# Two head groups of values behind one stationary operand, in a two-layer encoder trunk

## The chip, the cores and the metric

The kernel runs on one core of one Trainium2 chip. The metric is the time of one execution in microseconds (us): the median of several runs, and the lower the better. A profile of one execution stands beside it. Busy times, waits and the granted clock of TensorE come from that profile.

## What is computed

The reference is a bidirectional encoder of two layers with D_MODEL = 1024. It is run on two request groups that share all weights: 512 sample tokens and 256 prompt tokens, 768 columns together. Each layer projects the normalised input with one wide matrix and runs three token mixers on the result.

```python
z = h @ w_in
cq, ckv, kr, gate_a, qkv_b, gate_b, qkv_c, gate_c, merge = jnp.split(z, cuts, axis=-1)
o_a = mla_attention(cq, ckv, kr, g_q, w_uq, g_kv, w_ukv)
o_b = dilated_attention(rope(q_b, pos), rope(k_b, pos), v_b)   # three head groups, dilation 1, 4, 16
o_c = neighbourhood_attention(q_c, k_c, v_c, rpb)              # 8 heads on a grid 64 wide
mixed = mg[0] * (o_a * silu(gate_a)) @ w_pa + mg[1] * ... + mg[2] * ...
x = x + gate * rmsnorm(mixed @ w_out, g_post)
```

The change concerns the values of branch B (three head groups of four heads, so three times 256 columns of `w_in`) and of branch C (eight heads, taken as two groups of four, so twice 256 columns).

## The kernel before, in words

All matrix products are made in three passes of split operands: hi times hi, hi times lo, lo times hi. Activations `h` lie in SBUF as [feature, token], in eight tiles of 128 features (k = 0 to 7), each in a hi and a lo part. `feat_mm` (line 180) projects with the weights as stationary operand, and so yields features by tokens. One such projection is 8 x 3 x 2 = 48 matmuls, 24 with 512 columns (sample) and 24 with 256 (prompt).

Values are needed as tokens by features, so `value_group` (line 709) turns the roles round: 128 tokens are the stationary operand, and a group's 256 weight columns stream past. A group is 8 k x 6 token tiles x 3 passes = 144 matmuls (line 722). Six token tiles share three accumulators of 512 columns, two to one. `tok` picks the 128 tokens of a tile. For branch B with dilation 1 they are neighbours (`tok_b`, line 736). With dilation 4 and with dilation 16 they are every fourth token of the sample, or every second one of the prompt. These two picks are the same, since `strided` takes its step from the request group and not from the dilation. For branch C `tok_c` (line 886) has ScalarE write column-major copies `hc` of each k's hi and lo (line 893), 32 copies for one group, and the tiles are slices of these.

`load_split` (line 160) fetches 1024 weight columns and splits them: a ScalarE cast gives hi (line 175), a subtraction on VectorE or GpSimd gives lo (line 158). `store_v` (line 690) empties an accumulator into slots of tag `cv`: for each piece a ScalarE cast to hi (line 696), then a VectorE subtraction to lo (line 697). A group fills four slots, and there are 14 (`BUFS`, line 77). `vslice` (line 699) reads them in the products of probabilities and values (o_ps, lines 671, 859 and 872).

The projection accumulators come from pool `ps_mm`: three tiles of tag g0 and three of tag g1 may be in use at a time (`PS`, line 46). `feat_mm` takes one of each, `value_group` two g0 and one g1.

In a layer, `branch_a`, `branch_b`, `branch_c`, `merge` and `project` are traced in this order. `branch_b` makes its three value groups first (line 761). `branch_c` makes its first one before head pair 0 and the second before head pair 2 (line 924). The framework's planner then fixes the order of each engine's instructions by a simulation of its own, taking whatever is ready. So the tail of one branch runs mixed with the start of the next, and projections fill the time in which a softmax waits. `early` (line 990) adds merge gates as more such filling, by a table written by hand (`FILL`).

Of the kernel before, what the change touches and what calls it, by code (L numbers as in the profile page):

```python
# [11 lines left out]
F32 = mybir.dt.float32  # L12
F32R = mybir.dt.float32r
# [7 lines left out]
P = 128  # L21
D = 1024
KT = 8
NS, NP_ = 512, 256
# [36 lines left out]


@with_exitstack
def trunk_kernel(ctx, tc, x_t, c_row, c_col, w_ada0, w_ada, cols, w_a, w_feat, w_val, w_uqk, w_qr, w_uv, w_pj, w_o,
                 bias_s, bias_p, rope_t, rope_k, mask_b, mask_c, y_t):
    nc = tc.nc
    depth = w_feat.shape[0]
# [638 lines left out]
            s, c = b + 1, 256 + hd * 128  # L706
        return slots[s][:, c:c + 128]

    def value_group(l, idx, tok):

        slots = [U("cv", F32R, name="vb") for _ in range(4)]
        acc = [ps_mm.tile([P, NS], F32, tag=tag, name="vp") for tag in ("g0", "g0", "g1")]
        parts = []
        for k in range(KT):
            if k % 4 == 0:
                parts = load_split(w_val[l, idx, k // 4], 1024)[1]
            wh, wl = parts[(k % 4) // 2]
            ws = slice((k % 2) * 256, (k % 2) * 256 + 256)
            tk = tok(k)
            for t in range(6):  # L720
                for i, (a, w) in enumerate(((0, wh), (0, wl), (1, wh))):
                    nc.tensor.matmul(acc[t // 2][:, (t % 2) * 256:(t % 2) * 256 + 256], tk(t, a), w[:, ws],  # L722
                                     start=(k == 0 and i == 0 and t % 2 == 0),
                                     stop=(k == KT - 1 and i == 2 and t % 2 == 1))
        for t in range(6):
            store_v(slots, t, acc[t // 2][:, (t % 2) * 256:(t % 2) * 256 + 256])
        return slots


# [28 lines left out]
    def branch_b(l, h, hl):  # L758
        state["phase"] = "b"
        cos_b, sin_b = rope_tables(1)  # L760
        vb = [value_group(l, i, tok_b(h, d)) for i, d in enumerate((1, 4, 16))]
        o_t = None
        for hd in range(4):
            e = hd % 2
# [152 lines left out]

    def branch_c(l, h, hl):
        state["phase"] = "c"
        vc = None  # L920
        for pr in range(4):
            early(l, hl, FILL[l][13 + 2 * pr])
            if pr % 2 == 0:
                vc = value_group(l, 3 + pr // 2, tok_c(h))
            qo = feat_mm(w_feat[l, F_C + pr * 2], KT, hl, name="qc")
            qs2 = [q_stack(lambda g: qo[g], e, perm_cq, 0.125) for e in range(2)]
            ko = feat_mm(w_feat[l, F_C + pr * 2 + 1], KT, hl, name="kc")
# [319 lines left out]


def _value_tiles(w_in):
    starts = [1184 + 1536 + 256 * g for g in range(3)] + [3744 + 1024 + 256 * g for g in range(2)]  # L1250
    L = w_in.shape[0]
    out = [w_in[:, :, s:s + 256].reshape(L, 2, 4, P, 256).transpose(0, 1, 3, 2, 4).reshape(L, 2, P, 1024)
           for s in starts]
    return np.stack(out, 1)


def _chunk(w, cols):
# [62 lines left out]
def _layout(i):  # L1320
# [11 lines left out]
    uqn, uqr = uq[..., :64].reshape(L, 384, 512), uq[..., 64:].reshape(L, 384, 256)  # L1332
    uk, uv = ukv[..., :64].reshape(L, 256, 512), ukv[..., 64:].reshape(L, 256, 512)
    r = np.arange
    wuqk = np.stack([np.concatenate([_chunk(uqn, r(128) + 128 * j), _chunk(uk, r(128) + 128 * j)], 2)
                     for j in range(4)], 1)
    wqr = np.stack([_chunk(uqr, r(128) + 128 * j) for j in range(2)], 1)
# [7 lines left out]
    def spread(t):  # L1345
# [7 lines left out]
    mb, mc = _masks()  # L1353
    rope = _rope_tables()
    return dict(x_t=xt, c_row=crow, c_col=ccol, w_ada0=wada0, w_ada=wada, cols=colv.transpose(2, 0, 1), w_a=a["w_in"][:, :, :NA].reshape(L, KT, P, NA), w_feat=_feature_tiles(a["w_in"]),
                w_val=_value_tiles(a["w_in"]), w_uqk=wuqk, w_qr=wqr, w_uv=wuv, w_pj=wpj, w_o=wo,
                bias_s=bs, bias_p=bp, rope_t=rope, rope_k=_rope_rows(rope), mask_b=mb, mask_c=mc)


_NAMES = ["x_t", "c_row", "c_col", "w_ada0", "w_ada", "cols", "w_a", "w_feat", "w_val", "w_uqk", "w_qr", "w_uv", "w_pj", "w_o",  # L1360
          "bias_s", "bias_p", "rope_t", "rope_k", "mask_b", "mask_c"]


# [18 lines left out]
```

## Time and profile before

| | before |
|---|---|
| median of 3 runs | 2030.2 us (2030.12 to 2031.44) |
| the profiled execution | 2033.65 us |
| its span, first to last instruction | 2031.9 us |
| TensorE matmul busy | 1899.3 us, 93% |
| VectorE busy | 1548.6 us, 76% |
| ScalarE busy | 1066.2 us, 52% |
| mean granted TensorE clock | 0.977 |

A matmul's end is modelled in these profiles and the busy time of neighbours overlaps, so the pace of a run of matmuls is read from the starts: the time from the first start to the start of what follows, divided by their number. PE is the matmul, PEld the load of the stationary operand, DVE VectorE, ACT ScalarE, POOL GpSimd. In a window's row the granted clock of 1.00 is full speed and 0.50 the lower level.

### The profile page before, as it was taken

The numbers are of one execution on the slowest core, as the hardware profiler recorded it, in microseconds if no ns is written. First come the engines' busy times: TensorE is split into PE (matmuls) and PEld (weight loads), VectorE is DVE, ScalarE is ACT, GpSimd is POOL, SyncE is SP. The second block draws the span as 40 slices with busy tenths as digits, with TensorE's granted clock in tenths as the row PEclk, the third lists the DMA queues.
The fourth block names the chain that finished last, engine by engine and source line by source line (L and its number), as shares of the span: only waits on it lengthen the run. The fifth ranks groups of instructions, "written<-read, shape, count | busy, mean of one in ns | idle before, by whom it ended". The sixth has DMA issues, their size and how long they took to land.

```text
span 2031.9 us, 31377 instructions
## 1 busy us (share of the span) xinstructions
PE 1899.3 (93%) x11250; PEld 1706.7 (84%) x11250; DVE 1548.6 (76%) x3016; ACT 1066.2 (52%) x2185; POOL 641.3 (32%) x428
## 2 busy tenths in 40 slices
PE   7999899999989888999699999999999989898998
PEld 6987789988778777887699888889987878887898
DVE  8557787389978889799986258787489968888763
ACT  5456474256695855222264356574365586855241
POOL 6304334012113334125722014352012212434570
PEclk9999999999999998999899999999999999899999
DMA  8232231232312233557432242421232322233652
GB/s 286 72 115 67 92 110 57 71 93 76 96 43 71 89 123 104 176 168 263 154 117 72 88 129 85 134 77 59 73 91 73 99 66 86 82 112 107 207 176 76
DMA packets 94541, 220.28 MB, mean 108 GB/s; under 512 B 17984, under 2 KB 32392, under 8 KB 94384
## 3 DMA queue, kind: packets, MB, share of 16 engines
q1 hardware_dynamic: 89776, 211.97, 32.0%
q10 hardware_dynamic: 4608, 6.29, 1.1%
q8 instruction: 89, 1.46, 0.3%
q14 instruction: 68, 0.56, 0.1%
HBM read 172.73 MB, written 28.18 MB: 99 GB/s over the span
## 4 chain that ended last, share of the span: by engine, by line
PE 57%; DVE 25%; ACT 7%; issue 6%; DMA 3%; POOL 2%; SPq 0%; ACTq 0%; DVEq 0%; POOLq 0%
PE mg L199 14%; PE vp L722 8%; PE op L1133 6%; PE qkb L199 5%; PE pp L1032 5%; PE gate L199 4%; DVE fixed L158 3%; DVE fixed L309 3%; ACT hc L893 3%; PE cq L547 2%; DVE fixed L668 2%; PE sp L632 2%; PE ck L547 2%; PE o_ps L671 2%; DVE tq L658 1%
## 5 line engine op out<-in xcount | busy, mean ns | idle before, releaser
L653 POOL PARTITION_ALL_REDUCE fixed<-fixed x128 | 305.2, 2416 | 545.4 <-DVE fixed L650 325.7
L199 PE MATMUL mg<-fixed 128*128 128x512 f32 (+1 forms) x2304 | 433.2, 339 | 0.4 <-DVE kb L418 0.4
L199 PEld LDWEIGHTS mg<-fixed 128*128 128x128 f32 x2304 | 357.4, 189 | 49.8 <-PE sp L953 0.6
L175 ACT CAST fixed<-fixed 128x512 fp32r<-128x512 f32 (+1 forms) x332 | 199.6, 607 | 346.5 <-PE mg L199 106.6
L158 DVE TENSOR_TENSOR fixed<-fixed,fixed 128x512 fp32r<-128x512 f32 (+3 forms) x309 | 230.0, 747 | 147.2 <-ACT fixed L175 142.0
L199 PE MATMUL qkb<-fixed 128*128 128x512 f32 (+1 forms) x1152 | 211.3, 338 | 0.0
L199 PEld LDWEIGHTS qkb<-fixed 128*128 128x128 f32 x1152 | 176.4, 188 | 23.9
L199 PE MATMUL gate<-fixed 128*128 128x512 f32 (+1 forms) x960 | 185.1, 343 | 6.7 <-DVE fixed L158 4.0
L1032 PE MATMUL pp<-hi,fixed 128*128 128x512 f32 (+1 forms) x640 | 165.2, 346 | 20.3 <-DVE fixed L158 7.3
L199 PEld LDWEIGHTS gate<-fixed 128*128 128x128 f32 x960 | 150.7, 192 | 28.4 <-DVE fixed L158 4.5
L722 PE MATMUL vp<-fixed 128*128 128x256 f32 x864 | 154.6, 333 | 0.0
L722 PEld LDWEIGHTS vp<-fixed 128*128 128x128 f32 x864 | 153.1, 255 | 1.7
L1032 PEld LDWEIGHTS pp<-hi,fixed 128*128 128x128 f32 x640 | 113.8, 194 | 38.3 <-DVE fixed L158 9.4
L668 DVE TENSOR_TENSOR fixed<-tq,fixed 128x512 fp32r<-128x512 f32 (+1 forms) x160 | 130.6, 840 | 2.7 <-ACT fixed L667 2.4
L309 DVE SCALAR_TENSOR_TENSOR fixed<-tm,fixed 128x768 f32<-128x768 f32 (+1 forms) x128 | 109.1, 852 | 2.5 <-DMA tm<-in_w_ada_dram 0.4
L1032 PE MATMUL pp<-lo,fixed 128*128 128x512 f32 (+1 forms) x320 | 110.2, 345 | 0.0
L1133 PE MATMUL op<-wo,fixed 128*128 128x384 f32 (+1 forms) x648 | 107.9, 320 | 1.0 <-DVE fixed L1106 1.0
L659 ACT ACTIVATE tq<-tq 128x512 f32<-128x512 f32 (+1 forms) x160 | 82.6, 545 | 49.2 <-DVE tq L658 48.5
L893 ACT CAST hc<-fixed 128x512 fp32r<-128x512 f32 (+1 forms) x128 | 104.6, 894 | 0.2
L1133 PEld LDWEIGHTS op<-wo,fixed 128*128 128x128 f32 x648 | 102.1, 189 | 1.3 <-DVE fixed L1106 1.3
L658 DVE TENSOR_TENSOR tq<-tq,fixed 128x512 f32<-128x512 f32 (+1 forms) x160 | 98.1, 661 | 4.9 <-POOL fixed L653 4.5
L424 POOL MEMSET kb<- 64x768 f32 x56 | 41.1, 736 | 191.1 <-PE sp L790 58.2
(242 smaller groups left out, 3872.2 us busy)
## 6 DMA issues: line engine op xcount, KB each, us to landing
fixed<-in_w_feat_dram SPq DMA_DIRECT2D x108, 512.0 KB
tm<-in_w_ada_dram SPq DMA_DIRECT2D x42, 384.0 KB
th_scr<-the SPq DMA_DIRECT2D x35, 384.0 KB
th<-th_scr SPq DMA_DIRECT2D x35, 384.0 KB
fixed<-in_w_val_dram SPq DMA_DIRECT2D x20, 512.0 KB
xs<-xb SPq DMA_DIRECT2D x96, 96.0 KB
fixed<-in_w_pj_dram SPq DMA_DIRECT2D x32, 256.0 KB
fixed<-in_w_o_dram SPq DMA_DIRECT2D x16, 512.0 KB
```

What stands on the lines that cost most here:

```text
L158: eng.tensor_sub(out, a, b)
L175: nc.scalar.copy(hi[:, :m], raw[:, o:o + m])
L199: state["mm"] = nc.tensor.matmul(outs[g], w[:, wsl], a[g], start=(i == 0 and wi == 0), stop=(i == nk - 1 and wi == 2))
L309: nc.vector.scalar_tensor_tensor(junk, x, 1.0, c, ALU.mult, ALU.mult, accum_out=ada2[:, l, i, g, j:j + 1])
L653: nc.gpsimd.partition_all_reduce(red, out, P, RED.max if op == ALU.max else RED.add)
L658: nc.vector.tensor_sub(x, x, m)
L659: nc.scalar.activation(x, x, AF.Exp)
L668: nc.vector.tensor_sub(lo, x, f(hi))
L722: nc.tensor.matmul(acc[t // 2][:, (t % 2) * 256:(t % 2) * 256 + 256], tk(t, a), w[:, ws], start=(k == 0 and i == 0 and t % 2 == 0), stop=( ...
L893: nc.scalar.copy(x[:, o:o + n].rearrange("p (c r) -> p c r", r=rows), colmajor(f(h[i][g][:, k]), rows))
L1032: nc.tensor.matmul(pp, w[:, ws], o[k][a][:, o_:o_ + n], start=(i == 0), stop=(i == 3 * nk - 1))
L1133: mm = nc.tensor.matmul(op[cc], m[a][g][:, k, c0:c0 + P], parts[k][cc][b], start=(k == 0 and i == 0), stop=(k == KT - 1 and i == 2))
```

## The change

The values of the dilation-4 and dilation-16 groups of branch B are projected together, and so are the two groups of branch C. A new function, `value_pair`, streams 512 weight columns past each stationary operand and takes all six tiles of `ps_mm`, one for each token tile. Its weights come as a new array, in four loads of 1024 columns (two k of 512) where two groups had two loads each (four k of 256). The dilation-1 group keeps `value_group`. In branch C both groups are made before head pair 0, from one set of `hc` copies, and eight `cv` slots are filled then.

```diff
+    def value_pair(l, which, tok):
+
+        slots = [[U("cv", F32R, name="vb") for _ in range(4)] for _ in range(2)]
+        acc = [ps_mm.tile([P, NS], F32, tag=tag, name="vp") for tag in ("g0", "g0", "g0", "g1", "g1", "g1")]
+        parts = []
+        for k in range(KT):
+            if k % 2 == 0:
+                parts = load_split(w_val2[l, which, k // 2], 1024)[1]
+            wh, wl = parts[k % 2]
+            tk = tok(k)
+            for t in range(6):
+                for i, (a, w) in enumerate(((0, wh), (0, wl), (1, wh))):
+                    nc.tensor.matmul(acc[t], tk(t, a), w, start=(k == 0 and i == 0), stop=(k == KT - 1 and i == 2))
+        for t in range(6):
+            for j in range(2):
+                store_v(slots[j], t, acc[t][:, j * 256:j * 256 + 256])
+        return slots
...
-        vb = [value_group(l, i, tok_b(h, d)) for i, d in enumerate((1, 4, 16))]
+        vb = [value_group(l, tok_b(h, 1))] + value_pair(l, 0, tok_b(h, 4))
...
-        vc = None
+        vcs = None
         for pr in range(4):
             early(l, hl, FILL[l][13 + 2 * pr])
-            if pr % 2 == 0:
-                vc = value_group(l, 3 + pr // 2, tok_c(h))
+            if pr == 0:
+                vcs = value_pair(l, 1, tok_c(h))
+            vc = vcs[pr // 2]
```

The host lays the same weight columns out in the two arrays `w_val` and `w_val2`. The numbers computed are the same.

## Rows read from the trace of the kernel before

**Rows 1.** The page: TensorE's share, then busy tenths and granted clock in 40 slices.

```profile
PE 1899.3 (93%) x11250; PEld 1706.7 (84%) x11250; DVE 1548.6 (76%) x3016; ACT 1066.2 (52%) x2185; POOL 641.3 (32%) x428
...
PE   7999899999989888999699999999999989898998
...
PEclk9999999999999998999899999999999999899999
```

**Rows 2.** The chain that ended last, share of the span by line (page).

```profile
PE mg L199 14%; PE vp L722 8%; PE op L1133 6%; PE qkb L199 5%; PE pp L1032 5%; PE gate L199 4%; DVE fixed L158 3%; DVE fixed L309 3%; ACT hc L893 3%; PE cq L547 2%; DVE fixed L668 2%; PE sp L632 2%; PE ck L547 2%; PE o_ps L671 2%; DVE tq L658 1%
```

**Rows 3.** Stretches: length, busy us of each engine (instructions), granted clock, DMA share, GB/s.

```profile
324.98:385.33 60.35, 60.35 (x313) 59.90 (x312) 28.10 (x54) 16.98 (x40) 12.55 (x6) 1.00 0.17 56
1384.05:1444.23 60.18, 60.18 (x313) 59.80 (x312) 27.66 (x53) 17.29 (x40) 12.55 (x6) 1.00 0.15 52
470.00:530.00 60.00, 57.13 (x348) 50.12 (x348) 54.94 (x97) 38.12 (x69) 11.43 (x7) 1.00 0.28 87
563.00:600.00 37.00, 29.66 (x201) 26.57 (x200) 23.90 (x42) 35.78 (x51) 7.07 (x4) 0.95 0.10 36
672.00:705.00 33.00, 30.30 (x207) 27.92 (x208) 25.16 (x47) 29.97 (x46) 12.01 (x6) 0.94 0.27 86
1649.00:1681.00 32.00, 26.93 (x189) 24.29 (x190) 23.69 (x42) 28.11 (x45) 8.50 (x4) 1.00 0.15 50
1735.00:1773.00 38.00, 32.49 (x212) 30.41 (x211) 32.91 (x55) 34.57 (x56) 16.69 (x7) 0.87 0.23 77
```

**Rows 4.** TensorE's matmuls in 324.98 to 385.33, shapes kept apart.

```profile
L722 PE MATMUL vp<-fixed 128*128 128x256 f32 x290 | 58.7, 356 | 0.0
L671 PE MATMUL o_ps<-fixed,va 128*128 128x512 f32 x15 | 5.1, 395 | 0.0
L671 PE MATMUL o_ps<-fixed,va 128*128 128x256 f32 x8 | 1.9, 282 | 0.0
```

**Rows 5.** TensorE in order of time, merged: start us, us, engine, line, operation, count.

```profile
311.44 10.12 PE L722 MATMUL vp<-fixed 128*128 128x256 f32 x83
321.39 0.40 PE L671 MATMUL o_ps<-fixed,va 128*128 128x512 f32 x1
...
359.24 26.25 PE L722 MATMUL vp<-fixed 128*128 128x256 f32 x132
385.33 23.28 PE L199 MATMUL qkb<-fixed 128*128 128x512 f32 x133
```

**Rows 6.** The same view of both TensorE queues around one 512-column matmul.

```profile
348.09 0.40 PE L671 MATMUL o_ps<-fixed,va 128*128 128x512 f32 x1
348.09 1.71 PEld L722 LDWEIGHTS vp<-fixed 128*128 128x128 f32 x7
...
348.32 1.68 PE L722 MATMUL vp<-fixed 128*128 128x256 f32 x7
```

**Rows 7.** The chain in order of time: start us, us, one whole merge gate.

```profile
824.51 8.48 PE mg L199 x48
```

**Rows 8.** The column-major copies: their group on the page, and what waited for them.

```profile
L893 ACT CAST hc<-fixed 128x512 fp32r<-128x512 f32 (+1 forms) x128 | 104.6, 894 | 0.2
...
  ACT hc L893: 15.6, 20
```

**Rows 9.** `store_v`: count, then shortest, median and longest duration in ns.

```profile
L696 ACT CAST vb<-vp x80: 258/323/397, 323.7 to 1787.6; 128x256 fp32r<-128x256 f32 x40, 128x128 fp32r<-128x128 f32 x40
L697 DVE TENSOR_TENSOR vb<-vp,vb x80: 267/348/425, 327.8 to 1791.0; 128x256 fp32r<-128x256 f32 x40, 128x128 fp32r<-128x128 f32 x40
```

**Rows 10.** In order of time: branch B's last value products and branch C's first projections.

```profile
602.50 0.40 ACT L696 CAST vb<-vp 128x256 fp32r<-128x256 f32 x1
...
609.05 0.27 ACT L696 CAST vb<-vp 128x128 fp32r<-128x128 f32 x1
...
616.35 0.72 PE L859 MATMUL o_ps<-fixed,vb 128*128 128x256 f32 x3 [1.28 <-DVE fixed L158]
...
617.32 7.33 PE L199 MATMUL kc<-fixed 128*128 128x512 f32 x24 [0.24 <-DVE vb L697]
...
647.12 0.51 PE L872 MATMUL o_ps<-fixed,vb 128*128 128x256 f32 x3
...
1702.70 0.52 PE L872 MATMUL o_ps<-fixed,vb 128*128 128x256 f32 x3
```

More of the change, by code (lines that the diff above doesn't have):

```diff
@@ L63, in trunk_kernel @@
 @with_exitstack
-def trunk_kernel(ctx, tc, x_t, c_row, c_col, w_ada0, w_ada, cols, w_a, w_feat, w_val, w_uqk, w_qr, w_uv, w_pj, w_o,
+def trunk_kernel(ctx, tc, x_t, c_row, c_col, w_ada0, w_ada, cols, w_a, w_feat, w_val, w_val2, w_uqk, w_qr, w_uv, w_pj, w_o,
                  bias_s, bias_p, rope_t, rope_k, mask_b, mask_c, y_t):
@@ L707, in vslice, with value_group @@
         return slots[s][:, c:c + 128]
-    def value_group(l, idx, tok):
+    def value_group(l, tok):
         slots = [U("cv", F32R, name="vb") for _ in range(4)]
@@ L715, in value_group @@
             if k % 4 == 0:
-                parts = load_split(w_val[l, idx, k // 4], 1024)[1]
+                parts = load_split(w_val[l, k // 4], 1024)[1]
             wh, wl = parts[(k % 4) // 2]
@@ L1251, in _value_tiles @@
     L = w_in.shape[0]
-    out = [w_in[:, :, s:s + 256].reshape(L, 2, 4, P, 256).transpose(0, 1, 3, 2, 4).reshape(L, 2, P, 1024)
-           for s in starts]
-    return np.stack(out, 1)
+    one = w_in[:, :, starts[0]:starts[0] + 256].reshape(L, 2, 4, P, 256).transpose(0, 1, 3, 2, 4)
+    two = [np.concatenate([w_in[:, :, s:s + 256] for s in st], -1).reshape(L, 4, 2, P, 512).transpose(0, 1, 3, 2, 4)
+           for st in (starts[1:3], starts[3:5])]
+    return one.reshape(L, 2, P, 1024), np.stack([t.reshape(L, 4, P, 1024) for t in two], 1)
 def _chunk(w, cols):
@@ L1334, in _layout @@
     r = np.arange
+    wval, wval2 = _value_tiles(a["w_in"])
     wuqk = np.stack([np.concatenate([_chunk(uqn, r(128) + 128 * j), _chunk(uk, r(128) + 128 * j)], 2)
@@ L1355, in _layout @@
     return dict(x_t=xt, c_row=crow, c_col=ccol, w_ada0=wada0, w_ada=wada, cols=colv.transpose(2, 0, 1), w_a=a["w_in"][:, :, :NA].reshape(L, KT, P, NA), w_feat=_feature_tiles(a["w_in"]),
-                w_val=_value_tiles(a["w_in"]), w_uqk=wuqk, w_qr=wqr, w_uv=wuv, w_pj=wpj, w_o=wo,
+                w_val=wval, w_val2=wval2, w_uqk=wuqk, w_qr=wqr, w_uv=wuv, w_pj=wpj, w_o=wo,
                 bias_s=bs, bias_p=bp, rope_t=rope, rope_k=_rope_rows(rope), mask_b=mb, mask_c=mc)
-_NAMES = ["x_t", "c_row", "c_col", "w_ada0", "w_ada", "cols", "w_a", "w_feat", "w_val", "w_uqk", "w_qr", "w_uv", "w_pj", "w_o",
+_NAMES = ["x_t", "c_row", "c_col", "w_ada0", "w_ada", "cols", "w_a", "w_feat", "w_val", "w_val2", "w_uqk", "w_qr", "w_uv", "w_pj", "w_o",
           "bias_s", "bias_p", "rope_t", "rope_k", "mask_b", "mask_c"]
```

## The prediction, made before the changed kernel was run

> **What bounds the kernel now.** I read the page first, then the chain, then the stretches in which the changed code runs. TensorE is busy 93% of the span and its tenths stand at 8 or 9 nearly everywhere [rows 1]. The chain that ended last says the same by line: projections lead it, `vp` at line 722 (the value groups) has 8%, and the copies `hc` of ScalarE have 3% [rows 2]. A share is an average, so the stretches decide. While branch B's second and third group are projected, TensorE is busy for all of 60.35 us in layer 0 and all of 60.18 us in layer 1, at full granted clock (2.4 GHz), and VectorE for under half of it [rows 3]. Time taken off TensorE there comes off the end, as long as the next work is as dense, and it is: in the middle of branch B TensorE has 57.1 of 60 us and VectorE 54.9 [rows 3]. In branch C it is different. In the four stretches that hold its value groups TensorE is idle for 7.3, 2.7, 5.1 and 5.5 us, and ScalarE, which makes the copies, is busy for 35.8 of 37 us in the first [rows 3].
>
> **The pace of one value matmul.** The group with dilation 1 reads neighbouring tokens as its stationary operand: 83 matmuls start in the 9.95 us from 311.44 to 321.39, so 0.120 us each. With dilation 4 or 16 the tokens are strided: 132 in the 26.09 us from 359.24 to 385.33, so 0.198 us each, with the same 256 columns [rows 5]. What sets the second pace is therefore not the streaming of columns but the load of the strided operand. That is what the change can halve: two groups load the same strided tokens twice.
>
> **What a 512-column matmul will cost.** One merge gate is 24 matmuls of 512 columns and 24 of 256 in 8.48 us [rows 7]. That is 0.353 us for one of each. Taking off 0.120 leaves 0.233 us for the one with 512 columns and a contiguous operand. With a strided operand the question is whether its load still hides. Rows 6 have the nearest case: a 512-column matmul starts at 348.09, the load of a strided operand starts with it, and the next matmul starts at 348.32, which is 0.23 us later. The load ran wholly beneath the stream. I take 0.233 us for the strided pair also. The bounds are 0.233, where it hides, and 0.311, where the strided surplus of 0.198 - 0.120 = 0.078 us comes on top of the stream; the row nearest to the case is rows 6, and it gives the first.
>
> One rule speaks against this. The Trainium skill, page "TensorE: Matmul & The Clock Gate", Part 3, section "The mechanism", says that weight loads overlap matmuls in flight only when their row groups differ, and here all 128 rows are used by both. By that rule the pair would pay the load after the stream. The trace does not agree in the one place where it shows it [rows 6].
>
> **Branch B, per layer.** The stretch of 60.35 us holds the 288 strided matmuls and 23 of o_ps [rows 4]. The o_ps ones cost 15 x 0.233 + 8 x 0.120 = 4.5 us, which leaves 55.9 us (55.7 in layer 1, from 60.18 us with the same number of instructions). The pair is 144 x 0.233 = 33.6 us. Gain: 22.3 + 22.1 = 44.4 us for the two layers. The other edits there have one answer. Loads and splits of weights keep their number, and one load for 8.4 us of matmuls is the pace at which `feat_mm` already lives (one for 8.48 us). `store_v` keeps its 16 casts and 16 subtractions for two groups, about 5.2 and 5.6 us at the median durations [rows 9]. They come in one lump behind the pair instead of in two, beside VectorE that is less than half busy.
>
> **The six banks.** The pair holds every tile of `ps_mm`. Before, a group held three, so the next projection began at once: `qkb` starts 0.1 us behind the last value matmul [rows 5]. Now the next projection needs one g0 and one g1 tile back. The planner can run its 512-column half on the first g0 tile alone (24 x 0.233 = 5.6 us), while ScalarE and VectorE empty up to the fourth accumulator, ten pieces of some 0.35 us each. These begin while the last tokens are still streamed. Nothing in the trace shows all six held; by these rows it costs between 0 and 6 us at each pair. At the front of the pair the same holds for the tiles that the dilation-1 group leaves. I take 1.5 us for each layer's branch B, 3 us together. Behind the waiting projection the tail of branch A is still queued on TensorE and is not blocked, as it uses other accumulators.
>
> **Branch C, per layer.** Columns: 288 x 0.120 = 34.6 us become 33.6 us, so 1 us less per layer, 2 us in all. Copies: 64 of 128 go, half of 104.6 us of ScalarE [rows 8], but only what TensorE waited for counts. The two queues waited 15.6 us for them, counted twice where the load and its matmul waited together [rows 8]. The pair needs ScalarE's copies of one k for 18 x 0.233 = 4.2 us of matmuls instead of 18 x 0.120 = 2.2 us, against 104.6 / 32 = 3.3 us of copying per k. So copying stops setting the pace. The second stretch of each layer (33 and 38 us) goes as a place for value work, and with it part of its idle 2.7 and 5.5 us and of its half-clock time: granted 0.94 and 0.87 [rows 3] is half speed for 12% and 26% of these stretches, which costs 2 and 5 us. From idle and clock together I take 8 us for both layers. The bounds are 0, since softmax waits that are now filled by value work lose their filling, and 27.6 us, all of the four idle times and both clock losses.
>
> Against this stands the place where the pair ends. It wants eight `cv` slots of 14 while branch B's values still sit in 12. Before, two of four slots were free and the third store waited for a slot: the stores run at 602.50 and then at 609.05 [rows 10]. Branch B's last line-859 products, which free four slots, are at 616.35; its last products of all are at 647.12 in layer 0 and 1702.70 in layer 1 [rows 10]. Even before, `kc` waited for a store at 617.32 [rows 10]. With the pair the fourth accumulator, hence the first g1 tile, comes free only with the fifth and sixth slot, about 617. Until then TensorE has the g0 halves of `qc` and `kc`, 11 us. I take 5 us of waiting for both layers. Bounds: 0, and the rival below.
>
> **The sum.** -44.4 + 3 - 2 - 8 + 5 = -46.4 us. The profiled execution took 2033.65 us (span 2031.9 us), so it would be 1987.2 us. The median of the runs lies 3.4 us lower, which gives 1983.8 us; I say 1984.
>
> **The rivals.**
> - *The strided load does not hide.* The pair costs 144 x 0.311 = 44.8 us, branch B gains 11.1 and 10.9 us, and the total is 2030.2 - 24 = 2006. For it: every strided matmul in the trace streams 256 columns. Against it: rows 6.
> - *Branch C gives all that is idle there.* 27.6 us instead of 8, and none of the 5 us of waiting: 1984 - 25 = 1959 at the most, half of it 1971. For it: ScalarE is nearly full in its first stretch. Against it: VectorE is busy 25.2 of 33 and 32.9 of 38 us in the second stretches [rows 3] and loses nothing.
> - *Slower: the six banks stay locked until branch B ends.* If the planner gives the freed slots out so that no g1 tile can be emptied before branch B's last product, TensorE has nothing to project from the pair's end (563 + 33.6 + 57 other matmuls at 0.12 us = 604 in layer 0, so too about 1690 in layer 1) to 647 and 1703: 43 + 13 = 56 us, against a gain of 51 without the 5 taken above. The time would be 2030 + 5 = 2035, and the stall decides from 51 us. The Trainium skill ("PSUM — Partial Sum Buffer", "Specifications (TRN2)") gives the accumulator memory eight banks per partition; with six held, two are left for scores and o_ps, which would lengthen that tail. No row shows it. Against the rival: slots come free from 609 on [rows 10].
> - *No change*: the gain in branch B is given back further on because VectorE is as full there (54.9 of 60 us) as TensorE, 2030. Against it: VectorE's work of branch B begins with `qkb`, and this begins earlier.
>
> **How the numbers follow.** Forecast 0.68, with its own range 1972 to 1998. Branch C gives more 0.12; the load does not hide 0.09; locked banks 0.07; no change 0.04. The range of 1964 to 2008 holds the first three but for the far end of the second, and leaves out about 0.15. What a measurement here can tell from no change is 0.2%, 4 us: faster 0.89, same 0.04, slower 0.07.
>
> **What would show it.** In the changed profile the strided pair should run at about 0.23 us a matmul, dense from the dilation-1 group to `qkb`, some 34 us and the o_ps matmuls; at 0.31 the second case holds. `qkb` and `qc` should start within 2 to 3 us of the pair's end; an idle TensorE released by the `vb` stores, tens of us long around branch C's start, is the locked case. The copies must halve to 64, and head pair 2 of branch C should show no value matmul. I am wrong if branch B shortens by less than 35 us over both layers, or if branch C becomes longer.

## The result, and the profile after

The changed kernel takes 1973.6 us (median of 4 runs, 1972.72 to 1976.13), the kernel before 2030.26 us beside it. The ratio is 0.972, with an interval of 0.9705 to 0.9739, so 56.7 us are gone. The profiled execution took 1972.72 us with a span of 1970.9 us, 61.0 us less than the span before. The forecast was 1984 us, in a range of 1964 to 2008.

The page of the changed kernel, the lines that answer to [rows 1, 2]:

```profile
PE 1848.2 (94%) x10674; PEld 1641.7 (83%) x10674; DVE 1555.8 (79%) x3016; ACT 1016.3 (52%) x2121; POOL 645.1 (33%) x428
...
PE   7999899999989989998799999999999999988998
...
PEclk9999999999999989999899999999999999998999
...
PE mg L199 15%; PE qkb L199 6%; PE op L1152 6%; PE vp L741 4%; PE pp L1051 4%; PE gate L199 4%; DVE fixed L668 3%; DVE fixed L158 3%; PE cq L547 3%; DVE fixed L309 2%; PE sp L632 2%; PE ck L547 2%; DVE tq L658 2%; PE vp L722 2%; PE qc L199 2%
```

576 matmuls and 64 ScalarE instructions are gone. The value groups had 8% of the chain; now `value_pair` (line 741) has 4% and the dilation-1 group 2%. The copies `hc` had 3% and no longer appear in the line. The whole is as dense as before, at 94%.

The stretches in which the two pairs of branch B run, layer 0 and layer 1, with the columns of [rows 3], and the matmuls of the first one by form, as in [rows 4]:

```profile
322.50:361.25 38.75, 38.75 (x169) 36.02 (x168) 27.89 (x52) 15.89 (x36) 12.19 (x6) 1.00 0.26 86
1344.52:1383.20 38.68, 38.68 (x169) 36.00 (x168) 27.17 (x51) 15.94 (x36) 12.25 (x6) 1.00 0.24 83
...
L741 PE MATMUL vp<-fixed 128*128 128x512 f32 x144 | 36.4, 401 | 0.0
L671 PE MATMUL o_ps<-fixed,va 128*128 128x512 f32 x15 | 4.7, 394 | 0.0
L671 PE MATMUL o_ps<-fixed,va 128*128 128x256 f32 x8 | 2.1, 281 | 0.0
```

The same work took 60.35 and 60.18 us [rows 3]. TensorE has no idle time in either stretch and the granted clock is full. The end of the first pair in order of time, as in [rows 5]:

```profile
347.10 14.34 PE L741 MATMUL vp<-fixed 128*128 128x512 f32 x60
361.27 3.11 PE L199 MATMUL qkb<-fixed 128*128 128x512 f32 x13
```

Sixty matmuls start in 361.27 - 347.10 = 14.17 us, 0.236 us each. The next projection follows at that pace, with no wait for an accumulator.

To see where the time went, the span is cut at the first matmul of a kind. "Loss" is the length of a stage less the nominal time of its matmuls, 0.233 us for 512 columns [rows 7], 0.120 us for 256 [rows 5], and in proportion for other widths. So it holds idle time, time at the lower clock, and matmuls that start late. All numbers are us and worked out from the two traces.

| stage | before | after | difference | loss before | loss after |
|---|---|---|---|---|---|
| start to the first value matmul of B, layer 0 | 301.6 | 299.1 | -2.5 | 52.5 | 50.0 |
| value matmuls of B to `qkb`, layer 0 | 83.7 | 62.1 | -21.6 | 21.3 | 0.7 |
| `qkb` to the first output projection `op`, layer 0 | 588.8 | 574.0 | -14.8 | 73.0 | 59.2 |
| `op` of layer 0 to the value matmuls of B, layer 1 | 385.6 | 385.9 | +0.3 | 24.1 | 24.4 |
| value matmuls of B to `qkb`, layer 1 | 84.4 | 62.0 | -22.4 | 22.0 | 0.6 |
| `qkb` to `op`, layer 1 | 512.4 | 512.8 | +0.4 | 47.5 | 48.9 |
| `op` to the end | 75.2 | 74.9 | -0.3 | 6.1 | 5.8 |

Of 61 us, 44.0 come from the two value stretches of branch B. There the loss falls from 43 us to 1.3 us; the stream itself became only 1 us shorter per layer. The rest is nearly all in layer 0's stage that holds branch C. The first row shows what such a comparison can't resolve: nothing was changed there, but the planner's order shifts, and the stage differs by 2.5 us. In the twelve other runs below it lies between 299.1 and 301.3 us.

Branch C. Its copies, and what waited for whom, by the tile views of `hc` and `vp`; then `qc` behind the pair, layer 0 and layer 1, in order of time:

```profile
L911 ACT CAST hc<-fixed x64: 622/884/1183, 529.9 to 1621.8; 128x512 fp32r<-128x512 f32 x32, 128x256 fp32r<-128x256 f32 x32
  ACT hc L911: 9.2, 8
...
596.25 5.04 PE L199 MATMUL qc<-fixed 128*128 128x512 f32 x21 [1.61 <-DVE vb L697]
...
1628.08 0.28 PE L890 MATMUL o_ps<-fixed,vb 128*128 128x256 f32 x1
1628.20 4.95 PE L199 MATMUL qc<-fixed 128*128 128x512 f32 x21
```

The copies have halved and the waits for them went from 15.6 us [rows 8] to 9.2. `qc` waited 1.61 us for a store in layer 0 and not at all in layer 1, so the locked case did not happen.

The stages `qkb` to `op` as windows, before and then after:

```profile
385.33:974.16 588.83, 542.61 (x3171) 472.72 (x3170) 514.02 (x981) 311.83 (x578) 167.06 (x93) 0.97 0.36 117
1444.23:1956.60 512.37, 479.17 (x2882) 422.65 (x2881) 424.77 (x733) 301.37 (x562) 169.23 (x95) 0.98 0.33 106
```

```profile
361.27:935.30 574.03, 535.96 (x3027) 463.63 (x3026) 515.85 (x984) 287.65 (x549) 172.51 (x93) 0.97 0.37 121
1383.20:1896.00 512.80, 479.27 (x2737) 414.93 (x2736) 427.51 (x736) 277.61 (x533) 169.89 (x96) 0.98 0.33 106
```

In layer 0 TensorE is busy 6.7 us less and idle 8.1 us less (46.2 to 38.1). In layer 1 neither moved. ScalarE lost 24 us of copies in both, so copies alone can't explain a difference between the layers. Nor can the clock: its records of the layer 0 stage stand at the lower level for 34.1 us before and 37.5 after. And VectorE in layer 0 now has 515.85 of 574.03 us, 90%.

Times from the start of `qkb` (us), read from the starts of TensorE's instructions, for the kernels that the discussion needs:

| | first `qc` | first score of C | last score of C | last product with values | `op` |
|---|---|---|---|---|---|
| before, layer 0 / 1 | 203.0 / 216.8 | 248.5 / 259.2 | 393.7 / 402.8 | 433.7 / 439.3 | 588.8 / 512.4 |
| after | 235.0 / 245.0 | 262.1 / 271.5 | 379.7 / 396.6 | 418.9 / 442.1 | 574.0 / 512.8 |
| pair of C alone | 236.2 / 243.9 | 266.1 / 270.5 | 382.9 / 395.7 | 424.4 / 441.2 | 579.1 / 513.6 |
| 64 copies left out of before | 203.0 / 216.9 | 251.2 / 258.9 | 384.0 / 397.3 | 428.1 / 432.7 | 588.4 / 506.0 |
| 64 copies put back | 235.2 / 244.7 | 268.6 / 276.1 | 394.5 / 410.2 | 434.3 / 452.7 | 586.8 / 520.8 |
| scores ahead of the pair | 178.2 / 200.4 | 216.4 / 231.4 | 378.1 / 395.2 | 419.3 / 431.1 | 570.0 / 504.2 |
| pair in two passes | 229.9 / 246.2 | 269.3 / 273.5 | 387.3 / 397.5 | 426.2 / 427.1 | 580.9 / 499.7 |

Read it from right to left: `op` mostly moves with the last product, within 3 us. Before to after, layer 0: -14.8 and -14.8; layer 1: +2.8 and +0.4. The two exceptions are both in layer 0: with 64 copies left out of before the last product comes 5.6 us earlier and `op` 0.4, and with the scores ahead of the pair it comes 0.4 us later than after and `op` 4.0 earlier. And in both layers branch C starts its scores 12 to 14 us later than before, since the whole pair now stands in front of them, and makes that up later, when no value group interrupts head pair 2. In layer 0 the balance is a gain, in layer 1 it is nothing.

### The profile page after: what moved, and what is told of

Its sections match the earlier page's. It is cut to its first block, busy times and chain, and to the rows that moved or that the text cites. A ratio compares the mean times of both kernels' runs of the same rounds, so it can differ in the third digit from the quotient of the medians.

```text
span 1970.9 us, 30150 instructions
## 1 busy us (share of the span) xinstructions
PE 1848.2 (94%) x10674; PEld 1641.7 (83%) x10674; DVE 1555.8 (79%) x3016; ACT 1016.3 (52%) x2121; POOL 645.1 (33%) x428
## 4 chain that ended last, share of the span: by engine, by line
PE 58%; DVE 24%; issue 6%; ACT 5%; DMA 4%; POOL 2%; SPq 0%; DVEq 0%; ACTq 0%; POOLq 0%
PE mg L199 15%; PE qkb L199 6%; PE op L1152 6%; PE vp L741 4%; PE pp L1051 4%; PE gate L199 4%; DVE fixed L668 3%; DVE fixed L158 3%; PE cq L547 3%; DVE fixed L309 2%; PE sp L632 2%; PE ck L547 2%; DVE tq L658 2%; PE vp L722 2%; PE qc L199 2%
## 5 line engine op out<-in xcount | busy, mean ns | idle before, releaser
L653 POOL PARTITION_ALL_REDUCE fixed<-fixed x128 | 305.5, 2413 | 516.0 <-DVE fixed L650 317.4
L199 PE MATMUL mg<-fixed 128*128 128x512 f32 (+1 forms) x2304 | 439.2, 343 | 0.7 <-DVE u L435 0.5
L199 PEld LDWEIGHTS mg<-fixed 128*128 128x128 f32 x2304 | 363.0, 192 | 52.0 <-DVE u L435 0.9
L158 DVE TENSOR_TENSOR fixed<-fixed,fixed 128x512 fp32r<-128x512 f32 (+3 forms) x309 | 234.7, 764 | 96.5 <-ACT fixed L175 93.4
L199 PEld LDWEIGHTS qkb<-fixed 128*128 128x128 f32 x1152 | 176.9, 189 | 23.9
L856 POOL PARTITION_ALL_REDUCE fixed<-fixed x16 | 46.1, 2899 | 142.6 <-DVE fixed L833 75.2
L650 DVE TENSOR_TENSOR fixed<-tq 128x256 f32<-128x256 f32 (+1 forms) x128 | 78.2, 614 | 10.9 <-ACT tq L635 5.7
L667 ACT CAST fixed<-tq 128x512 fp32r<-128x512 f32 (+1 forms) x160 | 81.2, 531 | 8.8 <-PE o_ps L671 6.0
## 6 DMA issues: line engine op xcount, KB each, us to landing
tm<-in_w_ada_dram SPq DMA_DIRECT2D x42, 384.0 KB
th_scr<-the SPq DMA_DIRECT2D x35, 384.0 KB
th<-th_scr SPq DMA_DIRECT2D x35, 384.0 KB
```

What stands on the lines that cost most here:

```text
L158: eng.tensor_sub(out, a, b)
L199: state["mm"] = nc.tensor.matmul(outs[g], w[:, wsl], a[g], start=(i == 0 and wi == 0), stop=(i == nk - 1 and wi == 2))
L653: nc.gpsimd.partition_all_reduce(red, out, P, RED.max if op == ALU.max else RED.add)
L667: nc.scalar.copy(hi, x)
```

## The experiments

Every kernel was timed beside the kernel before. Four of them shared a group, and the change had one of its own, so kernels of different groups are compared by their ratios.

| kernel | time (us) | before in its group | ratio, interval |
|---|---|---|---|
| the change | 1973.6 | 2030.26 | 0.9722 (0.9705 to 0.9739) |
| pair in B alone | 1985.06 | 2032.99 | 0.9759 (0.9744 to 0.9774) |
| pair in C alone | 2020.69 | 2032.99 | 0.9940 (0.9925 to 0.9955) |
| before, neighbouring tokens | 1987.45 | 2032.99 | 0.9775 (0.9758 to 0.9793) |
| after, neighbouring tokens | 1974.36 | 2032.99 | 0.9709 (0.9695 to 0.9724) |
| C's pair in 256 columns | 1980.7 | 2031.63 | 0.9744 (0.9728 to 0.9761) |
| 64 copies put back | 2003.23 | 2031.63 | 0.9856 (0.9841 to 0.987) |
| a merge gate moved in both layers | 1976.24 | 2031.63 | 0.9725 (0.9711 to 0.974) |
| C's pair behind the first projections | 1988.04 | 2031.63 | 0.9782 (0.9767 to 0.9797) |
| scores ahead of the pair | 1965.77 | 2031.8 | 0.9674 (0.966 to 0.9689) |
| C's pair in two passes | 1970.16 | 2031.8 | 0.9700 (0.9684 to 0.9717) |
| a merge gate moved in layer 1 | 1970.51 | 2031.8 | 0.9699 (0.9685 to 0.9714) |
| before, 64 copies left out | 2022.69 | 2031.8 | 0.9958 (0.9942 to 0.9975) |

### The two halves of the change

The pair in branch B alone, with branch C as before:

```diff
-            if pr == 0:
-                vcs = value_pair(l, 1, tok_c(h))
-            vc = vcs[pr // 2]
+            if pr % 2 == 0:
+                vc = value_group(l, 3 + pr // 2, tok_c(h))
```

> Only branch B's dilation-4 and dilation-16 groups are made as a pair; branch C keeps two groups of 256 columns, each with its own copies, as before. Theory 1 (the gain is the strided operand loaded once instead of twice, on a full TensorE): the stretch from the first strided matmul to the first qkb shrinks by about 21.5 us per layer, as it did in the changed kernel (60.3 to 38.8 us), and all of it reaches the end: 2030.3 - 43 = 1987 us. Theory 2 (part of the 57 us comes from how the two edits meet, or branch B's shorter stretch is given back in branch C, where VectorE is the fuller engine): 1995 us or more.

Measured: 47.9 us faster than before, as theory 1 has it; theory 2 is out. The two value stretches take 62.1 and 62.9 us, together 43.1 us less than before (44.0 in the table of stages above), and `qkb` to `op` is 2.5 and 1.2 us shorter.

The pair in branch C alone, with branch B as before:

```diff
-        vb = [value_group(l, tok_b(h, 1))] + value_pair(l, 0, tok_b(h, 4))
+        vb = [value_group(l, i, tok_b(h, d)) for i, d in enumerate((1, 4, 16))]
```

> Only branch C is made as a pair with one set of copies; branch B keeps three groups of 256 columns, as before. Theory 1 (branch C's gain is real and stands by itself: half-clock time, idle time and copies go with the second value stretch): 2030.3 - 14 = 2016 us, 15 us of it in layer 0 and none in layer 1, as the stretches of the changed kernel show. Theory 2 (the extra 10 us over the forecast is luck of the planner's order after branch B's edit): 2030.3 - 5 = 2025 us, the forecast's own sum for branch C, or no gain at all.

Measured: 12.3 us faster than before, near theory 1. The halves add up to 60.2 us and the change gave 56.7; the intervals are some 3 us wide on either side. In this run too the gain is in layer 0 (579.1 us against 588.8) and not in layer 1 (513.6 against 512.4).

### Is it the strided load?

If what B gained was the strided load, it must also vanish where the load isn't strided and nothing is paired. The kernel before, with all groups of B on neighbouring tokens:

```diff
-        vb = [value_group(l, i, tok_b(h, d)) for i, d in enumerate((1, 4, 16))]
+        vb = [value_group(l, i, tok_b(h, 1)) for i in range(3)]
```

> The kernel before, with all three value groups of branch B reading neighbouring tokens (the dilation-1 pick), so the values of the two dilated groups stand in another token order than the reference wants. Nothing else changes: 256 columns, three accumulators. Theory 1 (the load of a strided operand sets the pace of 0.198 us, streaming takes 0.120): the two groups fall from 55.9 to 34.5 us per layer, and the kernel takes 2030.3 - 43 = 1987 us. Rival (256-column matmuls are slow there for another reason, such as the o_ps products between them or the weights' splits): the pace stays near 0.2 us and the time within 5 us of 2030.

Measured: 45.5 us faster than before, with value stretches of 62.3 and 62.3 us. The 132 matmuls that stood at 0.198 us each [rows 5] are now these, in order of time:

```profile
346.29 16.00 PE L722 MATMUL vp<-fixed 128*128 128x256 f32 x132
362.12 23.72 PE L199 MATMUL qkb<-fixed 128*128 128x512 f32 x133
```

That is 15.83 us for 132, 0.120 us each: the same instructions, the same widths, only another token step. So the surplus of 0.078 us per matmul belongs to the step, and without it there is nothing for a pair in branch B to gain but 1 us per layer.

The mean of 0.198 us hides two paces. Read start by start, 90 of the 132 matmuls before follow at 0.230 to 0.235 us and 42 at 0.115 to 0.127 (mean 0.122). They come mostly in runs of twelve slow and six fast ones, and that is the order of the code: per k four sample tiles, whose tokens lie at a step of four, then two prompt tiles at a step of two, three matmuls each. So the step of four costs 0.113 us a matmul, and the step of two costs as good as nothing. The loads of the same matmuls, before and in this run (count, then shortest, median and longest in ns), say so too:

```profile
L722 PEld LDWEIGHTS vp<-fixed x132: 194/329/332, 359.1 to 385.1; 128*128 128x128 f32 x132
...
L722 PEld LDWEIGHTS vp<-fixed x132: 187/189/191, 346.2 to 361.9; 128*128 128x128 f32 x132
```

The other side, the changed kernel with B's pair on neighbouring tokens:

```diff
-        vb = [value_group(l, tok_b(h, 1))] + value_pair(l, 0, tok_b(h, 4))
+        vb = [value_group(l, tok_b(h, 1))] + value_pair(l, 0, tok_b(h, 1))
```

> The changed kernel with its branch B pair reading neighbouring tokens, so the dilated groups' values stand in another token order than the reference wants. Theory 1 (a strided load hides wholly beneath 512 streamed columns): 144 matmuls at 0.233 instead of 0.236 to 0.239 us, at most 1 us per layer less, 1972 us. Rival (part of the strided load still shows): more than 3 us per layer less, below 1968 us.

Measured: ratio 0.9709 against 0.9722 of the change, inside each other's intervals. The last 60 matmuls of the pair, in order of time:

```profile
346.59 13.79 PE L741 MATMUL vp<-fixed 128*128 128x512 f32 x60
360.22 24.67 PE L199 MATMUL qkb<-fixed 128*128 128x512 f32 x140
```

13.63 us for 60 is 0.227 us each, against 0.236 with the step. Of the surplus of 0.078 us, 0.009 is left beneath 512 columns; the value stretches are 60.5 and 61.2 us against 62.1 and 62.0. The load hides, but with nothing to spare: at the step of four the loads alone paced the matmuls before at 0.233 us, which is as long as 512 columns take. A larger step was not run.

### Where branch C's gain is from

C's pair with the same operands and copies, but two matmuls of 256 columns for each of 512:

```diff
+                    for j in range(2):
+                        nc.tensor.matmul(acc[t][:, j * 256:j * 256 + 256], tk(t, a), w[:, j * 256:j * 256 + 256],
```

> The changed kernel, with branch C's pair streaming 2 x 256 columns past each stationary operand instead of 512: 288 matmuls again, but one set of copies and the same six accumulators. Theory 1 (with a contiguous operand the columns set the pace, 0.120 us for 256 and 0.233 for 512, so in branch C the wider matmul itself gives nothing): the time of the changed kernel within 3 us, 57 us below the kernel before. Rival (fewer matmuls and fewer operand loads are also worth something in branch C): 5 us or more slower than the changed kernel.

Measured: ratio 0.9744 against 0.9722, some 4.5 us slower, with intervals that overlap; that is between theory 1 (within 3 us) and the rival (5 us or more). The trace has `qkb` to `op` at 576.4 us in layer 0 and 516.9 in layer 1, 2.4 and 4.1 us more than after, of which 1 us each is the stream by the nominal times. The width is a small part; the layer 0 gain stays without it.

The changed kernel with a second, unused set of copies, as many as before:

```diff
+            elif pr == 2:
+                again = tok_c(h)
+                for k in range(KT):
+                    again(k)
```

> The changed kernel with the second set of column-major copies put back: before head pair 2 ScalarE writes all 32 copies of each layer once more, and nothing reads them. Theory 1 (most of branch C's gain is ScalarE's 52 us of copies, which stood in the softmax chain of the head pairs there): 8 to 12 us of the gain in layer 0 go again, about 46 us below the kernel before. Theory 2 (branch C's gain comes from the value matmuls, their half-clock time and their banks being out of the second stretch; ScalarE has room): at most 3 us slower than the changed kernel.

Measured: 1.34% of 2031 us, 27 us slower than the change, more than every expectation. It isn't a clean undoing: nothing holds the copies back, so the planner ran the 32 extra ones of a layer from 596 to 636 us and from 1646 to 1686 us, about the first scores of head pair 0 (629.9 and 1676.8 us) and not beside head pair 2. Most of the pair's own 32 copies and all the extra ones of layer 0 lie in 540 to 640 us and take more than half of ScalarE's time there, by line:

```profile
L911 ACT CAST hc<-fixed 128x512 fp32r<-128x512 f32 (+1 forms) x62 | 52.0, 898 | 0.9 <-PE sp L808 0.7
```

TensorE's own waits for copies hardly moved:

```profile
L911 ACT CAST hc<-fixed x128: 622/895/1215, 529.9 to 1685.7; 128x512 fp32r<-128x512 f32 x64, 128x256 fp32r<-128x256 f32 x64
...
  ACT hc L911: 9.3, 9
```

9.3 us against 9.2, and yet `op` is 12.8 and 8.0 us later than after in the two layers, and the scores of branch C start 6.5 and 4.6 us later (table of starts). The other 6.4 us of the longer span lie behind `op`, in stages in which nothing was changed. How the copies delay the scores stands in ScalarE's order of time, the casts of q (`qs`) in this run and then after:

```profile
604.35 1.77 ACT L911 CAST hc<-fixed 128x512 fp32r<-128x512 f32 x2
605.93 0.58 ACT L404 ACTIVATE qs<-qc 64x448 fp32r<-64x448 f32 x1
...
622.61 0.38 ACT L404 ACTIVATE qs<-qc 64x256 fp32r<-64x256 f32 x1
```

```profile
602.14 0.54 ACT L404 ACTIVATE qs<-qc 64x448 fp32r<-64x448 f32 x1 [0.62 <-PE qc L199]
...
612.23 0.38 ACT L404 ACTIVATE qs<-qc 64x256 fp32r<-64x256 f32 x1
```

`qkb` starts at the same time in both (361.3 us), yet the first of these casts is 3.8 us later and the last 10.4. ScalarE takes them one by one behind the copies; a copy in front of a cast of q or k delays the chain although no matmul waits for that copy. Counting only the waits that name `hc` misses this.

So the opposite was run too: the kernel before, in which the second group of C reads neighbouring tokens without copies, in the same place.

```diff
-                vc = value_group(l, 3 + pr // 2, tok_c(h))
+                vc = value_group(l, 3 + pr // 2, tok_c(h) if pr == 0 else tok_b(h, 1))
```

> The kernel before, in which branch C's second value group (head pair 2) reads neighbouring tokens straight from the activations, without its 64 column-major copies per run of eight k for both layers (32 per layer); its values then stand in another token order. Matmuls, their 256 columns, their contiguous loads, the accumulators and the place of the group stay as before, so only the copies go. Theory (the copies and not the 512 columns are what the change gained in branch C): the 12.3 us that branch C's pair alone gained come back here in whole, 10 to 20 us faster than before, most of it in layer 0. If only what TensorE waits for counts (half of the waits of 15.6 us, counted twice): 3 to 4 us. If the gain of branch C came from the wider stream: within 2 us of before.

Measured: 9.1 us faster than before by the medians, but not where the theory put it. `qkb` to `op` is 588.4 us in layer 0, 0.4 less, and 506.0 in layer 1, 6.4 less. And the granted-clock records of that stage of layer 1 stand at the lower level for 6.8 us, against 17.1 before, which is 5.1 us of work and most of the 6.4. The pair of C alone has 30.7 us of it there. So the 64 copies are not shown to be worth 9 us in themselves, and they don't explain layer 0. There the step that is left is the move, alone or together with the missing copies: with the second group ahead of head pair 0, beside the tail of branch B, head pairs 2 and 3 run through, and the last score is at 379.7 us instead of 393.7. That the move did it is what remains after the width and the copies by themselves; no run made it alone, so it is argued and not shown.

### What the move costs, and a kernel that takes it back

First, the pair of C traced behind `qc`, `kc` and the gate of head pair 0:

```diff
             early(l, hl, FILL[l][14 + 2 * pr])
+            if pr == 0:
+                vcs = value_pair(l, 1, tok_c(h))
+            vc = vcs[pr // 2]
             o_t = U("go", name="o_t")
```

> The changed kernel with branch C's pair traced behind the projections of head pair 0 (qc, kc, gate) instead of ahead of them. Theory 1 (in layer 1 branch C ends by its softmax chain, and the longer pair delays the start of that chain: the first scores of head pair 0 come 66 us after the first value matmul instead of 54): the chain starts earlier, and layer 1's branch C ends 8 to 12 us earlier, layer 0's by some us as well; 8 to 18 us below the changed kernel. Rival (branch B's tail sets the start of the chain, or the values are then late for head pair 0's products): within 4 us of the changed kernel, or slower.

Measured: 12 us slower than the change by the ratios. The projections do go first (`qc` at 178.1 and 206.3 us), but the scores, traced behind the pair, still start at 255.2 and 271.7, 6.9 us earlier than after in layer 0 and where they were in layer 1. Nothing was won: `op` is 3.5 and 10.7 us later than after. What makes it slower the run doesn't show.

Then the scores of head pair 0 were traced ahead of the pair as well, and the softmax and products behind it:

```diff
+            if pr == 0:
+                both = [scores(e) for e in range(2)]
+                vcs = value_pair(l, 1, tok_c(h))
+                vc = vcs[0]
+                for e in range(2):
+                    products(e, both[e])
```

> The changed kernel, but in head pair 0 of branch C the q and k projections and the scores of both heads are traced first, then the value pair, then softmax and products. Theory (the pair delays the softmax chain of branch C, since the scores now wait behind 33.6 us of value work; this is what gives layer 1 its gain back): the first scores of head pair 0 start within 20 us of the first C instruction instead of 54 to 84 us behind the first value matmul, the pair runs beneath the softmax, and branch C up to the first output projection shortens from 395.9 and 307.6 us by 5 to 15 us in each layer, 10 to 25 us in all. Rival 1 (the order is set by accumulators and not by the trace, as the run with the pair behind the gate already hinted, since six are held by the pair): the scores start where they did and the time is within 4 us of the changed kernel. Rival 2 (with the values late, the first products wait, and the tail of branch B, which used to lie beside the pair, loses its cover): slower than the changed kernel by 5 to 15 us.

Measured: 1965.77 us, ratio 0.9674, its interval (0.966 to 0.9689) below that of the change (0.9705 to 0.9739): 9.7 us faster by the ratios and 7.6 by the profiled spans, the fastest kernel of this study. The scores start 46 and 40 us earlier than after, and the stage is 4.0 and 8.6 us shorter. So of the delay that the pair puts in front of the softmax about a fifth at most was on the path. In layer 0 the last score moved by 1.6 us only. Windows of `qkb` to `op`:

```profile
362.68:932.72 570.04, 537.31 (x3026) 466.02 (x3025) 514.22 (x979) 287.46 (x550) 166.37 (x93) 0.97 0.38 121
1384.15:1888.36 504.21, 474.93 (x2738) 413.44 (x2737) 421.11 (x736) 277.54 (x533) 165.85 (x95) 0.99 0.34 108
```

VectorE is at 90% in the layer that gained less and at 84% in the other. In layer 1 TensorE's idle time fell from 33.5 to 29.3 us and the time at the lower clock from 23.9 to 13.7 us, which is 5.1 us of work; together 9.3 us for the 8.6. So more than half of layer 1's gain stands in the clock, and whether the earlier scores brought that about is not shown. This run also shows the wait that the prediction had priced and the change avoided. Layer 1 in order of time, the end of the pair with nothing else left to do:

```profile
1615.57 0.28 PE L969 MATMUL sp<-qs,ka 128*128 128x256 f32 x1
...
1647.71 8.45 PE L741 MATMUL vp<-fixed,hc 128*128 128x512 f32 x36 [1.24 <-ACT hc L911]
1660.06 0.50 PE L671 MATMUL o_ps<-fixed,vb 128*128 128x256 f32 x2 [3.89 <-DVE vb L697]
1661.36 6.82 PE L199 MATMUL qc<-fixed 128*128 128x512 f32 x22 [0.80 <-DVE vb L697]
```

The products wait 3.89 us for the first stores, and `qc` of the next head pair 0.80 us for an accumulator. In the changed kernel the products of branch B lie over the same place.

### Six accumulators

C's pair in two passes of three token tiles each: three accumulators at a time, 512 columns, one set of copies, but the weights fetched and split twice.

```diff
+        for first in (0, 3):
+            acc = [ps_mm.tile([P, NS], F32, tag=tag, name="vp") for tag in ("g0", "g0", "g1")]
...
+                for t in range(first, first + 3):
```

> The changed kernel, but branch C's pair is made in two passes of three token tiles: three accumulators at a time instead of six, still 512 columns per stationary operand and one set of copies, at the price of loading and splitting the weights twice (8 more casts of 512 columns on ScalarE and 8 more subtractions per layer, some 5 us of each). If the six held accumulators cost branch C some 8 us per layer (they keep the q and k projections of head pair 0 out until the pair ends): the projections start in the middle of the pair, and the time falls by about 5 us below the changed kernel in spite of the splits. If the accumulators cost nothing, as the start of the projections directly behind the pair suggests: no gain, and slower by 2 to 10 us through the splits on ScalarE and the second half's late copies.

Measured: ratio 0.9700, not apart from the change. The layers go opposite ways: `qkb` to `op` takes 580.9 us in layer 0 (6.9 more than after) and 499.7 in layer 1 (13.1 less). The projections gained little time: in layer 1 `qc` starts at 246.2 us, 1.2 later than after.

```profile
1632.96 5.44 PE L770 MATMUL vp<-fixed,hc 128*128 128x512 f32 x22
1638.24 0.85 PE L199 MATMUL qc<-fixed 128*128 128x512 f32 x4
```

So the mechanism that the theory named, projections in the middle of the pair, did not appear, and the gain of layer 1 has another cause. Idle time there fell by 10.1 us and the time at the lower clock by 17.1 us (8.5 us of work); what arranged that, the run doesn't tell. It stays open.

### Filling

A merge gate moved by hand ahead of head pair 2, where the second group used to stand; first in both layers (the 1 in place 17, counted from 0, for layer 0 too), then in layer 1 alone, which is the diff here:

```diff
-FILL = ((2, 0, 1, 0, 2, 3, 1, 0, 1, 1, 1, 1, 0, 0, 0, 0, 0, 0, 0, 0, 0), (5, 0, 2, 3, 0, 4, 0, 1, 1, 1, 1, 2, 1, 0, 0, 0, 0, 0, 1, 0, 0))
+FILL = ((2, 0, 1, 0, 2, 3, 1, 0, 1, 1, 1, 1, 0, 0, 0, 0, 0, 0, 0, 0, 0), (5, 0, 2, 3, 0, 4, 0, 1, 1, 1, 1, 2, 0, 0, 0, 0, 0, 1, 1, 0, 0))
```

> The changed kernel with the hand-written table of early merge gates altered for the hole that the second value group leaves: one gate more before head pair 2 of branch C in both layers; in layer 1 it is taken from the last head of branch B, in layer 0 from the merge. Theory 1 (branch C of layer 1 is bound by the softmax chain of its heads, while branch B is full on TensorE): a gate of 8.5 us that leaves branch B comes off the end there, and up to as much from the merge in layer 0: 5 to 12 us below the changed kernel. Rival (branch C has no room on TensorE): no change, or slower by up to 8 us.

Measured: 0.9725, the same as the change. In layer 0 `qkb` to `op` fell to 569.7 us, 4.3 less, and the stage behind it grew by 9.6 us (395.5 against 385.9). That stage holds the same matmuls in both kernels; its idle time is 3.7 us longer and its time at the lower clock 5.2 us, and why is not shown.

> The changed kernel with one entry of the hand-written filling table moved in layer 1 only: one merge gate that was a filling behind branch B's last head is put ahead of branch C's head pair 2, where the second value group used to stand. Theory (head pair 2 has lost its filling there): one merge gate is 8.5 us, so layer 1's stretch from qkb to branch C falls by 8 to 12 us, and branch C gives back less, since the gate fills idle time: 2 to 5 us faster than the changed kernel. Rival (TensorE has no idle time to fill there that another merge gate does not fill as well): within 2 us of the changed kernel.

Measured: 0.9699, 4.7 us faster by the ratios, but with overlapping intervals, so not apart from the change; its profiled span is 1971.7 us against 1970.9. In layer 1 the stage is 512.1 us against 512.8: up to branch C's first value matmul it is 10.4 us shorter, and behind it 9.7 longer. A gate fills the one place as well as the other.

## Why the prediction was right

The direction, the range and the main term held, and one term, branch C, was nearly three times too small. The measured 1973.6 us lies 1.6 us inside the range of 1972 to 1998 that the prediction gave its forecast. The place and the size of branch C's gain were not foreseen, so that the time did not fall below that range is luck.

- **The pace of the strided group, and what sets it.** Right. The reading of [rows 5], that the load of the strided operand and not the stream sets 0.198 us, is shown by the run with neighbouring tokens: 0.120 us with all else equal. What the reading missed is that 0.198 is a mean of 0.233 us at the step of four and 0.122 at the step of two. The sum is none the worse for it, as the pair has the same mix of tiles.
- **512 columns hide the load.** Right: 0.233 us was taken from [rows 6, 7], 0.236 was measured, and 0.227 without the step. The rival at 0.311 us is out. The sentence of the Trainium skill ("TensorE: Matmul & The Clock Gate", Part 3, "The mechanism") that a load overlaps matmuls in flight only when their row groups differ does not hold for these loads. By it the pair would have paid the load after the stream, and the pair paid 0.009 us of it. The same section also lets a load into the background weight buffer go ahead; which buffer a load went to, no run here shows.
- **Branch B's sum.** 44.4 us forecast, 44.0 in the trace, 47.9 (about 3 either way) in the run with this half alone.
- **The wait for six accumulators behind B's pair.** 3 us were taken, from 0 to 6 per pair; none is there, `qkb` starts 0.24 us behind the last value matmul. A price of the kind exists, 3.89 + 0.80 us, where nothing else is ready (scores ahead of the pair, layer 1).
- **Branch C.** This is the term that was mis-sized: -2 - 8 + 5 = -5 us forecast, -14.4 us in the trace, -12.3 us in the run with C's pair alone. Two steps failed. The 5 us of waiting for slots and accumulators was 1.6 us. And "only what TensorE waited for counts" is not a safe measure for the rest: 64 copies put back, in another place than before, cost 27 us, 20.8 of it in the two stages, while the waits that name `hc` stayed at 9.3 us. The 8 us were read from idle time in four windows around the value groups; the gain came at the end of the branch, by way of the last score and the last product, which those windows don't show. The two second stretches that were to go held more idle and lower-clock time in layer 1 (5.5 and 5 us) than in layer 0 (2.7 and 2), and the trace has the gain the other way round: 14.8 us in layer 0 and -0.4 in layer 1. Why layer 1 got nothing is partly shown at most: its scores start 12.3 us later, and the run that took this delay away gave 8.6 us, 5.1 of them in the clock. The rival in which branch C gives more, at half its size 1971 us, came nearer the measured time than 1984 did, but not by its mechanism, since the idle time that it counts lay in both layers.
- **Nothing given back.** The rival that VectorE gives the gain back is out for the change: no stage is longer by more than 0.4 us. But in layer 0, where VectorE is at 90%, starting the scores 46 us earlier gave only 4 us.

The forecast for the profiled execution was 1987.2 us and it took 1972.72. Of these 14.5 us, 9.4 are branch C, 3 the wait at B's pairs that is not there, and the rest is within what the planner's order moves.

## What to carry to other kernels

Compare the start-to-start time of equal matmuls with different operands before counting columns: where the pace depends on the operand's step, the load is the limit, and more columns per load are worth more than fewer instructions elsewhere. Look at single starts as well as at the mean, which can mix two paces. When work is moved to the front of a stage, look at the chain that it now stands in front of; the scores traced ahead of the pair gave nearly 10 us more. The wait that names a producer is not its whole price: on an engine that takes its instructions one by one, as ScalarE did here, the producer also delays what is queued behind it.

## What the runs showed of the hardware

- With a stationary operand of 128x128 fp32r whose tokens lie at a step of four, 256-column matmuls started every 0.233 us; at a step of two every 0.122 us, and with neighbouring tokens every 0.120 us. Under 512 columns the mix of the two steps took 0.236 us against 0.227 with neighbouring tokens.
- 512-column matmuls of one pair ran at 0.227 us, below the 0.233 us that a merge gate gives for them [rows 7].
- The granted clock of one and the same stage of layer 1 stood at the lower level for 6.8 to 30.7 us in kernels that differ little, 3.4 to 15.4 us of work; that of layer 0 did for 17.1 to 54.6 us. A difference of some 5 us in such a stage can be the clock alone.
